# Two layers of a hybrid attention trunk on one core: the dilated blocks taken two together, their scores four blocks ahead, and the output weights' splitting pinned behind the gates

## The chip, the cores and the metric

The kernel runs on one core of one Trainium2 chip. The metric is the device time in microseconds (us) of one execution. The engines are named as in the profile: PE is TensorE (PEld its weight loads), DVE is VectorE, ACT is ScalarE, POOL is GpSimd, and SP is SyncE, which here only issues DMAs. Each engine runs its own instructions in a fixed order and waits by semaphores for the others.

## The reference

What is computed, cut to what matters here (2048 positions, width 1024, two layers, float32):

```python
for layer in range(DEPTH):
    h = _rmsnorm(x, norm_g[layer])
    proj = einsum('bsd,dc->bsc', h, w_in[layer])
    qa, ka, va, ga, qd, kd, vd, gd = split(proj, cuts)
    oa = _stick_breaking(qa, ka, va) * silu(ga)          # 4 heads of 64
    qd, kd = rope(rmsnorm(qd)), rope(rmsnorm(kd))         # 12 heads of 64
    od = _dilated_mixture(qd, kd, vd) * silu(gd)
    x = x + concat([oa, od]) @ w_out[layer]

def _dilated_mixture(q, k, v):       # patterns (window, dilation): (128,1), (512,4), (2048,16)
    for window, dilation in DIL_PATTERNS:
        # blocks of 128 queries; keys: the block itself and the one before it
        s = q_block @ k_two_blocks / 8, masked to 0 <= dist <= window // dilation
        m = max(s); p = exp(s - m); l = sum(p)
        o = (p @ v_two_blocks) / l; log_den = m + log(l)
    alpha = softmax(stack(log_dens)); return sum(alpha * stack(outs))
```

## The kernel before

Each layer goes through four stages: the input projection, the stick-breaking heads, the dilated heads, and the output projection, which also begins the next layer. Matmuls that have to be exact split a float32 operand into a rounded part and the rest (cast, subtract) and add three products.

**The dilated stage** works on 6 pairs of heads. A pair has 48 blocks of 128 queries, 16 for each of the three patterns. In the first pattern, and for the first block of a sequence in the others, the keys are 128 wide, otherwise 256. A block `g` goes through three steps.

- `front(g)`: four score matmuls (L742) into one of the banks 0 to 2, then for each of two heads the mask and maximum on DVE (L744, out of the bank into a page of SBUF) and the exponential with its sum on ACT (L748).
- `mid(g)`: two or four transposes on PE (L763) into bank 3 or 4, then one copy to SBUF (L765), by ACT for `g % 4 == 1`, else by DVE.
- `back(g)`: once in four blocks, the products with the values (L777) into bank 5 and a copy by ACT into the pair's result page `o3` (L782, L784 or L787, by pattern).

The loop over `g` writes `front(g + 3)` ahead of `mid(g)`, and `back(g - 4)` behind it. PE's order is that of the program, since its instructions are pinned; on the other engines a scheduler decides where an instruction stands, by times of its own.

Beside this runs the mixing of the pair before. `stats_a` and `stats_b` (at `t = 1` and `t = 5`, where `t` is the block within the pair) make weights out of the three patterns' maxima and sums: five small POOL operations, one reciprocal on DVE (L832), four more on POOL (L833 to L836), which end in the tile `wr`. `weigh` then multiplies 128 positions by their weights: a matmul that reads `wr` (L847, called W below) and one DVE operation on its bank (L848). It is done for 16 chunks, one in each block from `t = 17`. `gate` adds the patterns and multiplies by the gate for four chunks at a time (three POOL operations of 128x512, L855, L856, L858), and `put` (L866) writes them to `mixa_l` in DRAM. Of the last pair, stats, weigh and gate follow only when all blocks are done, with the stats on DVE.

**The output stage** reads 7 of the 8 rows of `mixa_l` in slices of 128 positions (`load_m`: a DMA, L954, a cast on ACT, L957, and a subtract on DVE, L958) and multiplies them by the split output weights (L963, L966, L967; the three are called a step below). The weights come in 16 pieces of 128x512. `split(i)` casts a piece (L928; POOL for the first six, else ACT) and subtracts (L929, POOL). The first eight are loaded during the last blocks of the dilated stage; the other eight go into the page `G0`, which holds the `o3` of the last pair but one until its last `put` has landed (L945). The first two slices' steps fill PE until the last pair's `wr` is there: the first W of the last pair stands behind 12 steps.

## Time and profile before

| | |
|---|---|
| three runs, median (lowest, highest) | 3153.92 us (3147.05, 4272.47) |
| the profiled execution, its own time | 3151.59 us |
| its span, first to last instruction | 3149.9 us |
| mean granted TensorE clock, share of full | 0.993 |
| PE, DVE, ACT, POOL busy | 97%, 49%, 44%, 37% of the span |
| dilated stage, layer 0 and layer 1 | about 978 to 1376 us and 2545 to 2946 us |

The shares of the table are means over stages that have different limits. A timeline row gives the start, the length, the engine, the line, the tiles written and read, and in brackets how long the engine had been idle before it and what released it. PE's matmuls overlap, so the distance from one start to the next says what one costs, not its own length. The granted clock is 1.00 at 2.4 GHz and 0.50 at 1.2 GHz.

### The profile page before, as it was taken

To read this page: it belongs to the slowest core of one execution; us is meant where nothing else is said; L and a number is where in the kernel's file an instruction comes from. 1 tells how busy PE (TensorE), PEld (TensorE's weight loads), DVE (VectorE), ACT (ScalarE), POOL (GpSimd) and SP (SyncE) were. 2 spreads that over 40 slices of the span, in tenths; PEclk is the share of its full clock that TensorE was granted. 3 is DMA by queue.
4 is the path that set the end of the run, shared out by engine and by line. 5 is a ranking of instruction groups with operands and counts; after the bars stand their busy time and mean duration, and the time that the engine had idled before them with its cause. 6 is when DMAs were issued, how large, how long until landed. Compare 5 with 4: busy or idle time off the path is not lost.

```text
span 3149.9 us, 58168 instructions
## 1 busy us (share of the span) xinstructions
PE 3069.2 (97%) x21328; PEld 2615.0 (83%) x21328; DVE 1551.8 (49%) x4035; ACT 1370.4 (44%) x3917; POOL 1170.3 (37%) x1302
## 2 busy tenths in 40 slices
PE   8999999999999999979999999999999999999799
PEld 8888888887778988868898888888877789888687
DVE  6234430013777878864253243301147778888621
ACT  5222221113667888852042122211136688888410
POOL 1056651102663445451010666511036624445500
PEclk9999999999999999989999999999999999999899
DMA  6234456417123566354343344563172236663443
GB/s 200 89 102 121 112 137 199 136 53 227 58 81 95 154 192 176 104 163 145 124 144 104 97 110 119 148 205 119 59 219 61 72 95 177 190 174 102 137 146 99
DMA packets 316891, 413.10 MB, mean 131 GB/s; under 512 B 23232, under 2 KB 248512, under 8 KB 306368
## 3 DMA queue, kind: packets, MB, share of 16 engines
q1 hardware_dynamic: 314304, 405.20, 44.0%
q10 hardware_dynamic: 2304, 4.20, 0.4%
q8 instruction: 170, 2.79, 0.4%
q14 instruction: 113, 0.93, 0.1%
HBM read 252.01 MB, written 157.29 MB: 130 GB/s over the span
## 4 chain that ended last, share of the span: by engine, by line
PE 82%; issue 6%; ACT 4%; DVE 3%; DMA 2%; POOL 2%; SPq 1%; DVEq 0%; POOLq 0%; ACTq 0%
PE b L742 8%; PE b L317 7%; PE b L316 7%; PE b L315 7%; PE b L777 6%; PE b L763 6%; PE b L321 6%; PE b L323 6%; PE b L322 6%; PE b L599 4%; PE b L967 4%; PE b L966 4%; PE b L963 4%; PE b L585 2%; PE b L558 2%
## 5 line engine op out<-in xcount | busy, mean ns | idle before, releaser
L748 ACT ACTIVATE H<-H,T 128x256 f32<-128x256 f32 (+1 forms) x1152 | 519.4, 455 | 74.3 <-DVE T L744 67.8
L744 DVE CUSTOM_DVE_ANT_0 H<-b,M 128x256 f32<-128x256 f32 (+1 forms) x1152 | 370.9, 360 | 110.7 <-PE b L742 41.5
L742 PE MATMUL b<-F,F 128*128 128x256 f32 (+1 forms) x2304 | 408.4, 301 | 3.1 <-DVE T L744 3.1
L317 PE MATMUL b<-F,F 128*128 128x512 f32 (+1 forms) x1152 | 410.0, 356 | 0.5 <-DVE F L288 0.3
L573 POOL TENSOR_TENSOR G<-G 128x512 f32<-128x512 f32 (+3 forms) x320 | 287.7, 911 | 196.5 <-DVE G L567 143.2
L567 DVE TENSOR_TENSOR_SCAN G<-G,b 128x513 f32<-128x513 f32 (+3 forms) x320 | 323.8, 1079 | 73.2 <-ACT G L566 68.1
L742 PEld LDWEIGHTS b<-F,F 128*128 128x128 f32 x2304 | 312.1, 191 | 32.1 <-issue 26.3
L763 PE MATMUL b<-ident,H 128*128 128x128 f32 x1800 | 298.8, 277 | 7.8 <-ACT H L765 5.4
L315 PE MATMUL b<-F,G 128*128 128x512 f32 (+1 forms) x768 | 275.7, 359 | 0.4 <-ACT G L287 0.4
L316 PE MATMUL b<-F,G 128*128 128x512 f32 (+1 forms) x768 | 273.6, 356 | 1.5 <-POOL F L218 1.5
L315 PE MATMUL b<-F,F 128*128 128x512 f32 (+1 forms) x768 | 274.1, 357 | 0.0
L316 PE MATMUL b<-F,F 128*128 128x512 f32 (+1 forms) x768 | 272.3, 355 | 0.0
L317 PEld LDWEIGHTS b<-F,F 128*128 128x128 f32 x1152 | 217.6, 189 | 32.2 <-DVE F L288 1.1
L765 DVE COPY H<-b 128x512 f32<-128x512 f32 (+1 forms) x432 | 241.2, 558 | 4.3 <-PE b L763 4.1
L777 PE MATMUL b<-H,H 128*64 128x128 f32 x3600 | 235.7, 278 | 0.1
L763 PEld LDWEIGHTS b<-ident,H 128*128 128x128 f32 x1800 | 212.2, 141 | 17.7 <-ACT H L765 7.7
L322 PE MATMUL b<-F,F 128*128 128x512 f32 x576 | 224.6, 390 | 0.0
L566 ACT ACTIVATE G<-b 128x512 f32<-128x512 f32 (+3 forms) x320 | 163.9, 559 | 132.3 <-PE b L559 105.9
L777 PEld LDWEIGHTS b<-H,H 128*64 128x64 f32 x3600 | 192.8, 137 | 32.2 <-issue 21.9
L748 ACT ACTIVATION_READ_ACCUMULATOR H<-H,T 128x1 f32 x1152 | 219.5, 191 | 0.0
L135 POOL TENSOR_SCALAR U<-U 128x16 f32<-128x16 f32 (+1 forms) x80 | 18.9, 236 | 536.8 <-DVE U L367 316.3
L963 PE MATMUL b<-F,H 128*128 128x512 f32 x448 | 179.4, 400 | 29.3 <-ACT H L957 29.3
(159 smaller groups left out, 6297.0 us busy)
## 6 DMA issues: line engine op xcount, KB each, us to landing
qk_l<-H SPq DMA_DIRECT2D x384, 128.0 KB
F<-qk_l SPq DMA_DIRECT2D x48, 1024.0 KB
v_l<-S SPq DMA_DIRECT2D x288, 128.0 KB
H<-v_l SPq DMA_DIRECT2D x72, 512.0 KB
F<-qk_l SPq DMA_DIRECT2D x48, 512.0 KB
sq_l<-H SPq DMA_DIRECT2D x64, 256.0 KB
g_l<-S SPq DMA_DIRECT2D x64, 256.0 KB
F<-sq_l SPq DMA_DIRECT2D x32, 512.0 KB
```

The costliest lines, as they stand in the source:

```text
L315: nc.tensor.matmul(ps, hT(q, 0, k)[:, cs], wh, start=k == 0, stop=False)
L316: nc.tensor.matmul(ps, hT(q, 0, k)[:, cs], wl, start=False, stop=False)
L317: nc.tensor.matmul(ps, hT(q, 1, k)[:, cs], wh, start=False, stop=k == NK - 1)
L322: nc.tensor.matmul(ps, wh[:, w], hT(tq, 1, k), start=False, stop=False)
L567: nc.vector.tensor_tensor_scan(out=r[:, 0:n + 1][:, ::-1], data0=g[:, 512 - n:513][:, ::-1], data1=z[:, 0:1].to_broadcast([128, n + 1]), i ...
L573: nc.gpsimd.tensor_tensor(out=b[:, :n], in0=r[:, 1:n + 1], in1=r[:, 0:n], op=ALU.subtract)
L742: pin(nc.tensor.matmul(sc[:, h, :un], qb, kv, start=s == 0, stop=s == 1))
L744: nc.vector.tensor_tensor_reduce(out=pe[:, h, :un], in0=sc[:, h, :un], in1=mk[:, m0:m0 + un], scale=-0.125, scalar=3.0e38, op0=ALU.add, op ...
L748: nc.scalar.activation(pe[:, h, :un], pe[:, h, :un], AF.Exp, scale=-1.0, bias=st[:, 0, p, h, b:b + 1], accum_out=st[:, 1, p, h, b:b + 1])
L763: pin(nc.tensor.transpose(tp[:, ch, h], pe[:, h, 128 * w:128 * w + 128], ident))
L777: pin(nc.tensor.matmul(ob[64 * h:64 * h + 64, b % 4], vq[(pr * 3 + p) * 2 + (b - ch) // 8][:, (b - ch) % 8, 64 * h:64 * h + 64], ts[:, ch, h],
L963: ins = nc.tensor.matmul(ps, h, wo[k][:, 0, ns], start=k == 0, stop=False)
```

## The change

The loop of the dilated stage takes two blocks at a time: two `front`, four blocks ahead now; then W; then `back`, now ahead of `mid`; then two `mid`. In the first pattern the two blocks' transposes share one bank and one copy. The pages for the exponentials are six instead of five, those for the transposed ones four instead of five. W goes by a new timetable, with three chunks in four blocks (`t = 16` to 36), and for the last pair but one two in every two blocks (`t = 18` to 32). Gates follow their fourth chunk at once, and puts have new times.

In the output stage the six splits on POOL and all subtracts are pinned in the program's order. The first `load_m` is issued ahead of the late weights and its split ahead of theirs. The late weights come in another order, and the first steps take `k` 0 to 3 for both halves before `k` 4 to 6. Of the last pair's gates, those that DVE does are now the first and the third.

```diff
-    pe_s = Slices([pa[:, 0], pa[:, 1], pb[:, 0], pb[:, 1], tb[:, 512:1024].rearrange("p (h k) -> p h k", h=2)])
+    pe_s = Slices([pa[:, 0], pa[:, 1], pb[:, 0], pb[:, 1]]
+                  + [tb[:, i:i + 512].rearrange("p (h k) -> p h k", h=2) for i in (0, 512)])
...
-    ts_s = Slices([td[:, 0], td[:, 1], ta[:, 0], ta[:, 1], tb[:, 0:512].rearrange("p (c h q) -> p c h q", c=2, h=2)])
+    ts_s = Slices([td[:, 0], td[:, 1], ta[:, 0], ta[:, 1]])
...
     def mid(g):
...
+        both = g // 16 % 3 == 0
+        for i in range(2):
+            first = geom(g // 16 % 3, g % 16 + i)[2]
+            pe = pes.pop(g + i)
+            if i == 0 or not both:
+                tp, ts = t_r.get([128, 2, 2, 128]), ts_s.get()
...
+            if both and i == 0:
+                continue
+            on_act = g % 8 == 2 if both else (g + i) % 4 == 1
+            (nc.scalar.copy if on_act else nc.vector.tensor_copy)(ts[:, :lo + nch], tp[:, :lo + nch])
...
-        e1 = nc.vector if final and c4 % 2 else nc.gpsimd
+        e1 = nc.vector if final and c4 % 2 == 0 else nc.gpsimd
...
-    LEAD = 3
+    LEAD = 4
...
-        if g + LEAD < total:
-            front(g + LEAD)
-        if pr and 17 <= t < 33:
-            weigh(pr - 1, t - 17)
-            if t % 4 == 0:
-                gate(pr - 1, (t - 17) // 4)
-        mid(g)
-        if g % 4 == 0 and g:
-            back(g - 4)
+        if g % 2 == 0:
+            for i in (0, 1):
+                if g + LEAD + i < total:
+                    front(g + LEAD + i)
+            if pr:
+                cs = range(t - 18, t - 16) if pr == NPAIR - 1 else range(3 * (t - 16) // 4, 3 * (t - 14) // 4)
+                for c in cs:
+                    if 0 <= c < NT:
+                        weigh(pr - 1, c)
+                        if c % 4 == 3:
+                            gate(pr - 1, c // 4)
+            if g % 4 == 0 and g:
+                back(g - 4)
+            mid(g)
...
-            elif t in (26, 30, 34, 38):
-                put(pr - 1, (t - 26) // 4)
+            elif pr == NPAIR - 1 and t in (27, 31, 35, 38):
+                put(pr - 1, (t - 27) // 4 if t < 38 else 3)
+            elif pr < NPAIR - 1 and t in (25, 31, 35, 41):
+                put(pr - 1, (t - 25) // 5)
...
+    late = (8, 10, 12, 9, 11, 13, 14, 15)
...
+        if k < 3:
+            tc.keep_in_program_order(nc.gpsimd.tensor_copy(w[:, 0, ns], raw))
+        else:
+            nc.scalar.copy(w[:, 0, ns], raw)
+        tc.keep_in_program_order(nc.gpsimd.tensor_tensor(out=w[:, 1, ns], in0=raw, in1=w[:, 0, ns].bitcast(F32),
+                                                         op=ALU.subtract))
...
+    ms = [load_m(0)]
+    for j, i in enumerate(late):
+        raws[i] = ar[:, 2048 + 512 * j:2560 + 512 * j]
+        nc.sync.dma_start(out=raws[i], in_=w_l[:, i // 2, 512 * (i % 2):512 * (i % 2) + 512])
+    ms.append(load_m(1))
     yield
-    for i in range(8, 16):
+    m7 = yield
+    hl = [split_m(ms[0])]
+    for i in late:
         split(i)
-    m7 = yield
-    if proj:
-        proj.begin()
+    hl.append(split_m(ms[1]))
...
+        for ks in ((0, 1, 2, 3), (4, 5, 6)):
+            for n in range(2):
+                if ks[0] == 0:
+                    early[c, n] = acc.get([128, 512])
+                for k in ks:
+                    mms(early[c, n], mh, ml, c, k, slice(512 * n, 512 * n + 512), True)
+                    yield
+    if proj:
+        proj.begin()
```

In the changed file the lines have other numbers: scores L743, mask L745, exponential L749, transposes L767, their copy L772, products with the values L783, the copies into `o3` L790 and L793, reciprocal L838, the POOL operations behind it L839 to L842, W L853 and its DVE operation L854, gate L862 to L864, put L872, weight split L943, L945 (cast on POOL, on ACT) and L946, `load_m` L951, its cast and subtract L957 and L958, late weights L976.

**The first W of a pair.** On PE, in pair 1 of layer 0, the first W of pair 0 (its tile is read as `W`) stood behind one block's scores, before:

```order
L763 MATMUL b_1083_9625<-ident,H_772_7472 128x128 x2
...
L777 MATMUL b_1084_9629<-H_771_7471,H_1041_9350 64x128 x4
L742 MATMUL b_1085_9639<-F_949_8670,F_1003_9054 128x128
...
L847 MATMUL b_1087_9650<-W_7475,F_900_8376 128x384
L763 MATMUL b_1088_9653<-ident,H_769_7469 128x128 x4
L742 MATMUL b_1090_9661<-F_949_8670,F_1003_9054 128x256
```

After, it stands behind the scores of the blocks 20 and 21 (banks `b_1067` and `b_1068`) and ahead of the products with the values and the next transposes:

```order
L767 MATMUL b_1062_9577<-ident,H_770_7470 128x128 x4
L743 MATMUL b_1067_9593<-F_942_8663,F_996_9047 128x128
...
L743 MATMUL b_1068_9602<-F_942_8663,F_996_9047 128x256
...
L853 MATMUL b_1070_9613<-W_7475,F_900_8376 128x384
L783 MATMUL b_1071_9616<-H_771_7471,H_1033_9341 64x128 x8
L767 MATMUL b_1072_9626<-ident,H_772_7472 128x128 x2
L767 MATMUL b_1073_9630<-ident,H_772_7472 128x128 x4
```

On DVE, at the same pair, the reciprocal stood ahead of the masks of the blocks 12 to 20, with the first W's operation (L848 on bank `b_1087`) behind them, before:

```order
L765 COPY H_773_7473<-b_1060_9489 128x256
L832 RECIPROCAL X_7474<-X_7474 32x128
L744 ISA H_769_7469,T_1028_9254<-b_1062_9503,M_7467 128x128
...
L765 COPY H_772_7472<-b_1083_9625 128x256
...
L848 TENSOR_TENSOR G_905_8389<-G_905_8389,b_1087_9650 128x3x128
```

After, it stands behind the mask and maximum of block 21 (bank `b_1068`), and the next row is that W's operation (on bank `b_1070`):

```order
L772 COPY H_771_7471<-b_1062_9577 128x512
L745 ISA H_770_7470,T_1018_9214<-b_1067_9593,M_7467 128x128
...
L745 ISA H_770_7470,T_1018_9214<-b_1068_9602,M_7467 128x256
L745 ISA T_1018_9214 128x1
...
L838 RECIPROCAL X_7474<-X_7474 32x128
L854 TENSOR_TENSOR G_905_8389<-G_905_8389,b_1070_9613 128x3x128
L772 COPY H_773_7473<-b_1072_9626 128x256
```

So the reciprocal has come to the block whose scores stand right ahead of W on PE. It is the same in the pairs 3 and 5 (there one block later) and in both layers; in the pairs 2 and 4 it stands behind block 13, eight blocks ahead.

**The end of the dilated stage, POOL and SP.** On POOL, in layer 0, the gates of pair 4 (`G_1474`, the `o3` of that pair) stood among the splits of the weights, before:

```order
L855 TENSOR_TENSOR G_1474_12277<-G_1474_12277 128x512
L929 TENSOR_TENSOR F_1761_14229<-F_1741_14069,F_1761_14229 128x512
L929 TENSOR_TENSOR F_1750_14140<-F_1740_14064,F_1750_14140 128x512 x2
...
L858 TENSOR_TENSOR G_1474_12277<-G_1474_12277,S_1707_13854 128x512
L929 TENSOR_TENSOR F_1755_14176<-F_1741_14069,F_1755_14176 128x512
L856 TENSOR_TENSOR G_1474_12277<-G_1474_12277 128x512
L858 TENSOR_TENSOR G_1474_12277<-G_1474_12277,S_1722_13948 128x512
L496 MEMSET T_2378_20806 128x128
```

After, the four gates (now `G_1440`) stand ahead of all splits:

```order
L864 TENSOR_TENSOR G_1440_12189<-G_1440_12189,S_1664_13793 128x512
L862 TENSOR_TENSOR G_1440_12189<-G_1440_12189 128x512
L863 TENSOR_TENSOR G_1440_12189<-G_1440_12189 128x512
L864 TENSOR_TENSOR G_1440_12189<-G_1440_12189,S_1678_13885 128x512
L943 CAST F_1697_14002<-F_1695_13991 128x512
L946 TENSOR_TENSOR F_1697_14002<-F_1695_13991,F_1697_14002 128x512
...
L946 TENSOR_TENSOR F_1714_14142<-F_1696_13996,F_1714_14142 128x512 x2
L946 TENSOR_TENSOR F_1733_14290<-G_1719_14177,F_1733_14290 128x512
```

On SP, the two `load_m` stood behind the late weights, before:

```order
L866 DMA mixa_l_205<-G_1474_12277 128x512
L844 DMA S_1792_14455<-g_l_204 128x512
...
L635 DMA M_22679<-in_masks 128x732
L945 DMA G_1766_14264<-in_w_out 128x512 x8
L954 DMA G_1766_14264<-mixa_l_205 128x7x128 x2
L257 DMA X_14400<-in_norm_g 128x1024
```

After, the first stands ahead of them and the next behind, with the next layer's weights (L214) last:

```order
L872 DMA mixa_l_205<-G_1440_12189 128x512 x3
L850 DMA S_1741_14352<-g_l_204 128x512
L951 DMA G_1719_14177<-mixa_l_205 128x7x128
L976 DMA G_1719_14177<-in_w_out 128x512 x8
L951 DMA G_1719_14177<-mixa_l_205 128x7x128 x2
L214 DMA H_1767_14486<-in_w_in 128x4x256
...
L850 DMA S_1747_14384<-g_l_204 128x512
```

**The end of the dilated stage, ACT.** The end of ACT's row in layer 0, before, with the last exponentials ahead of all that waits for the late weights or for `mixa_l`:

```order
L748 ACTIVATE H_770_7470,T_1624_13286<-H_770_7470,T_1624_13286 128x256 x2
L787 COPY G_1623_13285<-b_1769_14288 128x4x16x8
L765 COPY H_773_7473<-b_1770_14306 128x512
L787 COPY G_1623_13285<-b_1773_14324 128x4x16x8
L820 COPY X_7474<-b_1777_14350 32x384
L217 CAST F_1784_14402<-H_1787_14408 128x1024
L820 COPY X_7474<-b_1778_14359 32x384
L217 CAST F_1784_14402<-H_1786_14404 128x1024
L828 ACTIVATE X_7474<-X_7474 32x384
L928 CAST F_1779_14380<-G_1766_14264 128x512 x2
```

After, the cast of the first slice and casts of late weights (`G_1719` is the page that the DMAs fill) stand among the exponentials of the last four blocks:

```order
L957 CAST H_1731_14286<-G_1719_14177 128x896
L945 CAST F_1733_14290<-G_1719_14177 128x512
L749 ACTIVATE H_770_7470,T_1582_13182<-H_770_7470,T_1582_13182 128x256 x4
L793 COPY G_1581_13181<-b_1711_14110 128x4x16x8
L945 CAST F_1733_14290<-G_1719_14177 128x512
L772 COPY H_773_7473<-b_1713_14134 128x512
L749 ACTIVATE H_772_7472,T_1582_13182<-H_772_7472,T_1582_13182 128x256 x3
L945 CAST F_1736_14305<-G_1719_14177 128x512
...
L945 CAST F_1734_14293<-G_1719_14177 128x512 x2
L772 COPY H_773_7473<-b_1722_14212 128x512
L793 COPY G_1581_13181<-b_1725_14230 128x4x16x8
L957 CAST H_1737_14310<-G_1719_14177 128x896
```

So on ACT the work that waits for DMAs has moved from behind the last copies to ahead of them.

## Rows read from the trace of the kernel before

**Rows 1.** The page: busy time of each engine, share of the span.

```profile
PE 3069.2 (97%) x21328; PEld 2615.0 (83%) x21328; DVE 1551.8 (49%) x4035; ACT 1370.4 (44%) x3917; POOL 1170.3 (37%) x1302
```

**Rows 2.** Stages: length, busy us of PE, PEld, DVE, ACT, POOL, then PEclk.

```profile
1126.70:1142.60 15.90, 15.90 (x155) 14.58 (x154) 15.13 (x60) 13.55 (x51) 6.65 (x6) 1.00 0.47 152
1376.00:1402.00 26.00, 8.48 (x32) 6.18 (x32) 10.22 (x14) 10.11 (x15) 11.30 (x10) 0.61 0.95 306
2946.00:2965.00 19.00, 6.47 (x18) 4.52 (x17) 8.37 (x13) 7.71 (x12) 11.68 (x8) 0.64 0.94 295
```

**Rows 3.** Timeline, PE, layer 1, last pair: start, length, line, idle before.

```profile
2919.87 0.79 PE L742 MATMUL b<-F,F 128*128 128x256 f32 x4
2920.49 0.60 PE L763 MATMUL b<-ident,H 128*128 128x128 f32 x4
2920.85 0.78 PE L742 MATMUL b<-F,F 128*128 128x256 f32 x4
2924.08 1.12 PE L763 MATMUL b<-ident,H 128*128 128x128 f32 x4 [2.45 <-ACT H L765]
2924.85 1.20 PE L742 MATMUL b<-F,F 128*128 128x256 f32 x4
2925.85 1.05 PE L763 MATMUL b<-ident,H 128*128 128x128 f32 x4
```

**Rows 4.** Timeline, ACT, the same stretch.

```profile
2920.94 0.62 ACT L928 CAST F<-F 128x512 fp32r<-128x512 f32 x1 [2.71 <-DMA F<-in_w_out]
```

**Rows 5.** Timeline, PE, end of the dilated stage of layer 0.

```profile
1393.85 0.77 PE L963 MATMUL b<-F,H 128*128 128x512 f32 x1 [16.96 <-ACT H L957]
...
1405.91 0.39 PE L967 MATMUL b<-F,H 128*128 128x512 f32 x1
1406.14 0.34 PE L847 MATMUL b<-W,F 128*128 128x384 f32 x1
```

**Rows 6.** Timeline, SP, the same end.

```profile
1375.76 0.46 SPq L866 DMA_DIRECT2D mixa_l<-G  x1
...
1381.24 3.79 SPq L945 DMA_DIRECT2D G<-in_w_out  x8
1385.17 1.52 SPq L954 DMA_DIRECT2D G<-mixa_l  x2
```

**Rows 7.** Timeline, POOL, the same end.

```profile
1366.34 1.29 POOL L858 TENSOR_TENSOR G<-G,S 128x512 f32<-128x512 f32 x1
...
1385.88 8.72 POOL L929 TENSOR_TENSOR F<-G,F 128x512 fp32r<-128x512 f32 x7 [9.16 <-ACT F L928]
```

**Rows 8.** Timeline, PE, end of the dilated stage of layer 1.

```profile
2958.76 0.77 PE L963 MATMUL b<-F,H 128*128 128x512 f32 x1 [12.33 <-ACT H L957]
...
2970.15 0.34 PE L847 MATMUL b<-W,F 128*128 128x384 f32 x1
```

**Rows 9.** Timeline, SP, the same end.

```profile
2936.44 10.34 SPq L844 DMA_DIRECT2D S<-g_l  x2
```

**Rows 10.** Timeline, DVE, layer 0, statistics of pair 0, in pair 1.

```profile
1118.96 0.94 DVE L832 RECIPROCAL X<-X 32x128 f32<-32x128 f32 x1 [1.42 <-POOL X L831]
```

**Rows 11.** Timeline, POOL, after that row.

```profile
1119.98 0.99 POOL L833 TENSOR_TENSOR X<-X 32x384 f32<-32x384 f32 x1 [1.05 <-DVE X L832]
...
1124.79 0.50 POOL L836 CAST W<-X 32x384 fp32r<-32x384 f32 x1
```

**Rows 12.** Timeline, PE, after that row.

```profile
1121.51 1.10 PE L777 MATMUL b<-H,H 128*64 128x128 f32 x16
1122.53 0.66 PE L742 MATMUL b<-F,F 128*128 128x128 f32 x4
...
1127.18 0.39 PE L847 MATMUL b<-W,F 128*128 128x384 f32 x1
```

**Rows 13.** Timeline, DVE, end of the dilated stage of layer 0.

```profile
1385.07 0.35 DVE L834 CAST W<-X 32x384 fp32r<-32x384 f32 x1
...
1386.03 1.32 DVE L836 CAST W<-X 32x384 fp32r<-32x384 f32 x1
```

More of the change, by code (lines that the diff above doesn't have):

```diff
@@ L919, in _output, with load_m, split_m @@
     acc = mem.bank_ring(0, 1, 2, 5)
-    wo, raws = [], []
+    wo, raws = {}, {}
     pages = ("F0", "F1", "F2", "F3", "F9", "F10", "F11", "F8")
+    late = (8, 10, 12, 9, 11, 13, 14, 15)
     def split(i):
         k, ns = i // 2, slice(512 * (i % 2), 512 * (i % 2) + 512)
-        if i % 2 == 0:
-            wo.append(mem.get(pages[k], [128, 2, DM], F32R))
+        if k not in wo:
+            wo[k] = mem.get(pages[k], [128, 2, DM], F32R)
         w, raw = wo[k], raws[i]
-        (nc.gpsimd.tensor_copy if k < 3 else nc.scalar.copy)(w[:, 0, ns], raw)
-        nc.gpsimd.tensor_tensor(out=w[:, 1, ns], in0=raw, in1=w[:, 0, ns].bitcast(F32), op=ALU.subtract)
+        if k < 3:
[4 more added lines that the diff above has]
+                                                         op=ALU.subtract))
+    def load_m(c):
+        m = m_s.get()
+        nc.sync.dma_start(out=m[:, 0:7], in_=mix[0][:, :, 128 * c:128 * c + 128].rearrange("k p t -> p k t"))
+        return m
+    def split_m(m):
+        mh = mh_r.get([128, 8, 128], F32R)
+        ml = ml_r.get([128, 8, 128], F32R)
+        nc.scalar.copy(mh[:, 0:7], m[:, 0:7])
+        nc.vector.tensor_tensor(out=ml[:, 0:7], in0=m[:, 0:7], in1=mh[:, 0:7].bitcast(F32), op=ALU.subtract)
+        return mh, ml
     for j in range(8):
@@ L967, in mms @@
         nc.tensor.matmul(ps, l, wo[k][:, 0, ns], start=False, stop=k == 7)
[L969 removed]
+    early = {}
     for c in range(2):
[L971 to L976 removed]
+        mh, ml = hl[c]
+        for ks in ((0, 1, 2, 3), (4, 5, 6)):
[7 more added lines that the diff above has]
+        proj.begin()
     for c in range(NT):
[L978 to L979 removed]
+        mh, ml = hl[c] if c < 2 else split_m(load_m(c))
         xt = x_s.get()
```

51 lines of the change are left out of this document (13 added, 38 removed).

## The prediction

> **What bounds the kernel now.** I read the page first: PE is busy 97% of the span, every other engine under half of it, PEld apart [rows 1]. So nothing that another engine saves counts unless PE waits for it. Next I read the stages, to find where PE does not work: 26 us after the dilated stage of layer 0 hold 8.48 us of PE at a granted clock of 0.61, and 19 us in layer 1 hold 6.47 at 0.64 [rows 2]. Then the timeline of PE inside the dilated stage: score matmuls and transposes alternate with 0.62 us from scores to transposes and 0.36 back [rows 3]. There PE is bound by its own issue, and what can be gained is the small waits and the alternation. The rest (the projection, the stick-breaking heads, most of the output) the change does not touch.
>
> **The end of the dilated stage (gain).** PE's last work before the gap ends at 1393.85 - 16.96 = 1376.89 us in layer 0; call it Z. The first W of the last pair starts at 1406.14, Z + 29.25 [rows 5]. In layer 1, Z is 2958.76 - 12.33 = 2946.43 and that W starts at Z + 23.72 [rows 8]. Ahead of that W stand 12 steps of three matmuls, 0.23 us apart at full clock [rows 5], 0.70 a step, 8.4 us in all. The rest is waiting and half clock. The chain in layer 0: the last gate ends at 1367.6, since splits lie between the gates [rows 7]; its put is issued at 1375.76, the late weights at 1381.24, the first slice only at 1385.17 [rows 6], and PE starts on its cast. In layer 1 SP stands in one issue from 2936.44 for 10.3 us ahead of all that [rows 9].
>
> After, the last gate has no split ahead of it. It takes three operations of 1.29 us [rows 7] behind a W that PE issues 12 blocks ahead of the end, and by my estimate (1.0 to 1.5 us a block, as the starts in rows 3 have it) it is done 14 us ahead of Z. A put then took 5.5 us until what waits for its landing was issued [rows 6]; with that and some 4 us for the slice, which now stands ahead of the late weights on SP, the slice has landed 4.5 to 7 us ahead of Z. So PE goes from the stats to the steps without a gap, and W of the last pair would start at Z + 8.4 in layer 1. In layer 0 ACT has two casts of the next layer's weights, whose DMAs are now issued last, ahead of the last pair's exponential; by my estimate W starts at Z + 11.1. Gains: 29.25 - 11.1 = 18.2 and 23.72 - 8.4 = 15.3, together 33.5 us. The half clock goes with the gap.
>
> **The same end (cost).** ACT works in order, and six casts of late weights and the cast of the first slice now stand ahead of the last exponentials and copies. Each waits for a DMA. The trace has such a wait: a cast waited 2.71 us for its weights, and PE sat idle 2.45 us for it [rows 3, 4]. With the slice landing 4.5 to 7 us ahead of Z and the weights behind it, the exponentials of the last four blocks come 2 to 4 us late. I take 3.0 us for each layer (between 0 and 6): 6.0 us. Net of the end: -27.5 us.
>
> **The first W in the pairs 1, 3 and 5 (cost).** This is the new wait. The reciprocal stands on DVE behind the mask of block 21 (22 in pair 5), and PE has W directly behind the scores of that block. Between them lie the last masks' end on DVE, the reciprocal, 0.94 us [rows 10], and four POOL operations, two of 1.0 and two of 0.5 us (one of each is shown) [rows 11]: 0.94 + 3.0 = 3.94, and with some 1.3 us for the two masks and the hand-overs 5.2 us; in pair 5, where PE has other work meanwhile, I take 4.7. What is queued behind W on PE is everything: products, transposes, the next scores. DVE stands behind it too, with W's own operation. Before, nothing waited there: `wr` was ready at 1124.79 + 0.50 and the first W came at 1127.18 [rows 11, 12]. Per layer 5.2 + 5.2 + 4.7 = 15.1 us, 30.2 in both.
>
> The clock follows. After 2.45 us of idle PE the same work took 0.77 instead of 0.36 us and 1.00 instead of 0.62 [rows 3]: two fifths of the stretch were lost. How long a spell lasts behind a longer gap no row here says to the microsecond; I take between 3.4 and 7 us behind each of the six waits, 1.3 to 2.9 us lost, 1.8 taken: 10.8 us.
>
> **The flow of the blocks (gain).** Taking two blocks together halves the changes between scores and transposes, from eight to four in four blocks. A round of scores and transposes takes 0.98 us, though four scores alone last 0.78 and four transposes 0.60 [rows 3], so they overlap and a change can cost little: I take 0.025 us (between 0 and 0.07), 0.10 for four blocks, 1.0 for the most of a pair. In the second pattern DVE is at 15.13 of 15.90 us [rows 2], and with three W in four blocks instead of four it has a quarter of its W operations less there; I take 1.0 us of PE's time for a pair (between 0 and 1.5). The reciprocal's wait before, for which DVE sat idle 1.42 us [rows 10], is gone in pairs 1, 3 and 5; of it and the reciprocal's 0.94 us I take 0.5 us as seen by PE. So -2.5 us for each of these; in pairs 2 and 4 the reciprocal stays and blocks DVE for as long as before, with the copies of two blocks behind it: -1.1; in pair 0, with no W and no reciprocal, -1.0. Per layer 3 x 2.5 + 2 x 1.1 + 1.0 = 10.7, in both 21.4 us.
>
> Edits with no price: the pages (one more for exponentials, one less for transposed blocks) only serve the order; the new puts stand on SP behind no DMA that PE waits for before the end; the shared copy of the first pattern saves DVE work in a stretch where PE waits for ACT and itself. ACT would then be nearly as full as PE there; if it does not keep up, the first pattern gives back some 0.3 us a pair.
>
> **A term the trace does not show.** Products now follow scores directly. No row has that sequence. The nearest is the reverse: 16 products and then scores take 1.02 us from start to start [rows 12], and at 0.055 us a product, from their length in the row, the last of them costs 0.20 us until the scores start. I take that for the new sequence, with bounds 0.09 below and above it. There are 144 of these in the run, so -13 to +13 us, 0 taken.
>
> **Sum.** -27.5 + 30.2 + 10.8 - 21.4 = -7.9 us against the profiled run's own 3151.6: 3143.7, say 3144. That run lies 2.3 us below the median of the three; I make no correction for it.
>
> **Rivals.** (1) *No wait at the first W.* If the weights are ready when PE comes to W, the two W terms vanish: 3151.6 - 27.5 - 21.4 = 3103. For it: the W of before had 1.9 us to spare, and a stall lets ACT catch up, which may return some of it. Against it: the order on PE, DVE and POOL is fixed, and the reciprocal stands behind the mask that itself waits for PE's last scores ahead of W. Chance 0.18.
>
> (2) *Slower: products behind scores are dear.* The place is each `back`, 144 times. At 0.29 us instead of 0.20 the flow's gain shrinks by 13 us and the time is 3157. It decides from 0.20 + 7.9 / 144 = 0.26 us on: beyond that the kernel is slower than before. For it: products and transposes read other pages and another format than the scores, and each change in PE's order seen so far costs something. Against it: the reverse costs 0.20 [rows 12]. Chance 0.13.
>
> (3) *POOL holds DVE at the end.* A cast of the stats on DVE that took 0.35 us took 1.32 when a row of POOL's subtracts began just ahead of it [rows 7, 13]. After, the late subtracts run on POOL from just ahead of Z to some 10 us behind it, and the last pair's stats, some eight DVE operations, fall in that time; if each second one loses 1 us, W of the last pair comes 4 us late in each layer, and the time is 3152, no change at all. For it: the row. Against it: in layer 0 most subtracts should be over by then. Chance 0.14. The Trainium skill, "SBUF — State Buffer", section "SBUF: two separate sides", has the rule for this: DVE and POOL share a port pair as an exclusive lock, and whichever starts first keeps it for the whole instruction. The row agrees with it (0.97 us lost, less than POOL's 1.29). It speaks against a change that gathers POOL's splits; by it the sum would be some 8 us higher, without it nothing.
>
> **How the numbers follow.** The forecast has 0.55 with a range of its own of 3130 to 3157. The range of 8 in 10 has to reach down into rival 1, at 3103 give or take 10, and up over rival 2: 3094 to 3166. A change of 2% is 63 us, about what a measurement of this kernel tells from none; 3091 and 3217 are the limits. Faster by more needs rival 1 with the end at its best (-33.5): 0.05. Slower by more needs all costs at their upper bounds and more: 0.02. Within: 0.93.
>
> **What would show it.** In the trace after: the first W (L853) of pairs 1, 3 and 5 with 4 to 6 us idle ahead of it, released by POOL L842, and a granted clock under 1 behind it; in pairs 2 and 4 none. PE idle under 2 us at Z, no stretch at 0.5 there, W of the last pair at Z + 8 to 11. Casts L945 and L957 on ACT waiting for DMAs ahead of the last exponentials, with PE idle 2 to 4 us ahead of Z. Pairs 2 and 4 shorter by some 1 us each. Wrong it would be above all if the first slice lands later than I reckon, for then the last exponentials, and all behind them, wait for it.

## The result, and the profile after

The changed kernel takes 3174.78 us (median of four runs, 3169.09 to 3180.91) against 3149.19 for the one before (median of three); the ratio is 1.0079, with an interval of 1.0052 to 1.0106. It is slower by 0.8%, where 3144 was forecast with a range that ended at 3166. A fourth run of before, at 4272.47 us, was a slow one and stands outside this comparison, though the median of 3153.92 in the table ahead still counts it. The profiled execution of after took 3175.19 us with a span of 3173.5, 23.6 more than the span before.

The page of after, busy time of each engine [rows 1 were before]:

```profile
PE 3071.5 (97%) x21328; PEld 2628.6 (83%) x21328; DVE 1545.8 (49%) x3963; ACT 1360.1 (43%) x3893; POOL 1172.8 (37%) x1302
```

PE is busy for 2.3 us more, the span is 23.6 longer: the rest, 21.3 us, is idle PE. So the list of PE's waits of after comes next (total, times, longest in us):

```profile
PE b L853 <- POOL W L842: 31.7, 6, 5.6
PE b L767 <- ACT H L772: 11.3, 10, 3.4
...
PE b L853 <- DVE W L842: 7.9, 2, 5.0
PE b L783 <- DMA H<-v_l: 5.4, 1, 5.4
```

Before, the head of this list was L963 on L957, 29.3 us in two waits, the gaps of [rows 5, 8]; that line is gone. The first line is the forecast wait at the first W of the pairs 1, 3 and 5 (30.2 us forecast). The second stood at 5.4 us before, so it has grown by 5.9. The third and the fourth were not in the forecast's sum.

**The first W**, pair 1 of layer 0, timeline of PE, DVE and POOL. (The captions of [rows 10 to 12] say pair 1; those rows lie in pair 2, which begins at 1102.6 us. The argument is the same in each pair.)

```profile
1057.85 1.17 PE L743 MATMUL b<-F,F 128*128 128x128 f32 x8
1064.65 0.69 PE L853 MATMUL b<-W,F 128*128 128x384 f32 x1 [5.62 <-POOL W L842]
1065.26 1.98 PE L783 MATMUL b<-H,H 128*64 128x128 f32 x16
1067.17 1.54 PE L767 MATMUL b<-ident,H 128*128 128x128 f32 x6
```

```profile
1060.42 0.94 DVE L838 RECIPROCAL X<-X 32x128 f32<-32x128 f32 x1
```

```profile
1053.53 2.29 POOL L687 CAST F<-F 128x512 fp32r<-128x512 f32 x4
1055.78 0.44 POOL L837 TENSOR_TENSOR X<-X 32x128 f32<-32x128 f32 x1
1061.43 0.98 POOL L839 TENSOR_TENSOR X<-X 32x384 f32<-32x384 f32 x1 [5.21 <-DVE X L838]
...
1064.10 0.49 POOL L842 CAST W<-X 32x384 fp32r<-32x384 f32 x1
```

The reader is to see two things. The reciprocal had its input at 1056.2 and stood ready for 4.2 us behind masks; then the chain over POOL takes 3.2 us, with PE behind it. And ahead of L837 POOL ran four casts of the third pattern's queries, 2.29 us together, which the forecast did not look at.

The stretch behind this wait, a window of after (length, busy us of PE, PEld, DVE, ACT, POOL, then PEclk):

```profile
1064.60:1068.60 4.00, 3.95 (x24) 3.30 (x25) 0.98 (x2) 0.59 (x1) 0.00 (x0) 0.50 0.03 7
```

The granted clock fell to 0.50, its lower level, behind the 5.62 us of idle PE. The 16 products behind W take 1.91 us there from their start to the next, where 16 took 1.02 in [rows 12].

**Pair 3 of layer 0.** PE's timeline, the chain of waits ahead of it (start, length, what), and SP's timeline; below them the row of SP for the same load before:

```profile
1198.66 1.73 PE L783 MATMUL b<-H,H 128*64 128x128 f32 x13 [5.43 <-DMA H<-v_l]
```

```profile
1175.93 22.59 DMA H<-v_l
```

```profile
1171.26 0.32 SPq L663 DMA_DIRECT2D F<-qk_l  x1
1171.67 0.45 SPq L664 DMA_DIRECT2D F<-qk_l  x1
1172.17 2.54 SPq L665 DMA_DIRECT2D F<-qk_l  x1
1174.81 0.54 SPq L663 DMA_DIRECT2D F<-qk_l  x1
1175.40 0.45 SPq L664 DMA_DIRECT2D F<-qk_l  x1
1175.93 0.54 SPq L697 DMA_DIRECT2D H<-v_l  x1
1176.52 9.64 SPq L665 DMA_DIRECT2D F<-qk_l  x1
```

```profile
1168.20 1.51 SPq L696 DMA_DIRECT2D H<-v_l  x1
```

The load of the values for pair 3 stands on SP behind five of the six loads of queries and keys; before it stood behind three. It is issued 69.5 us behind the start of pair 2, where it was 65.6. It took 22.59 us to land, and PE waited for it.

**The end**, both layers, timeline of PE. The steps now follow the statistics without a gap (Z is 1405.15 and 2984.39), but W waits behind them:

```profile
1405.15 0.50 PE L987 MATMUL b<-F,H 128*128 128x512 f32 x1
...
1418.82 0.66 PE L853 MATMUL b<-W,F 128*128 128x384 f32 x1 [5.01 <-DVE W L842]
...
2984.39 0.50 PE L987 MATMUL b<-F,H 128*128 128x512 f32 x1
...
2995.99 0.42 PE L853 MATMUL b<-W,F 128*128 128x384 f32 x1 [2.93 <-DVE W L842]
```

So W comes at Z + 13.7 and Z + 11.6, instead of Z + 29.25 and Z + 23.72 [rows 5, 8]. POOL and DVE at the same place in layer 0, to be read against [rows 7, 13]:

```profile
1380.54 1.27 POOL L864 TENSOR_TENSOR G<-G,S 128x512 f32<-128x512 f32 x1
...
1409.58 8.30 POOL L946 TENSOR_TENSOR F<-G,F 128x512 fp32r<-128x512 f32 x6 [4.90 <-ACT F L945]
```

```profile
1411.32 1.26 DVE L836 TENSOR_TENSOR X<-X 32x128 f32<-32x128 f32 x1
1412.61 1.26 DVE L837 TENSOR_TENSOR X<-X 32x128 f32<-32x128 f32 x1
1413.91 0.94 DVE L838 RECIPROCAL X<-X 32x128 f32<-32x128 f32 x1
...
1415.46 1.30 DVE L840 CAST W<-X 32x384 fp32r<-32x384 f32 x1
1416.80 1.50 DVE L841 TENSOR_TENSOR X<-X,W 32x384 f32<-32x384 f32 x1
```

POOL's row of six subtracts lies over the last pair's statistics, and four of DVE's operations take 1.26 to 1.50 us. The loads, SP, against [rows 6]:

```profile
1385.62 0.37 SPq L951 DMA_DIRECT2D G<-mixa_l  x1
1386.04 4.60 SPq L976 DMA_DIRECT2D G<-in_w_out  x8
```

The last gate now ends 23 us ahead of Z, at 1381.8 (forecast: 14; before: 9), and the first slice is issued at 1385.62, ahead of the late weights.

Ahead of Z, PE waits for ACT, whose copy stands behind exponentials and casts, in layer 1 (PE, then ACT):

```profile
2973.48 0.91 PE L767 MATMUL b<-ident,H 128*128 128x128 f32 x4 [3.41 <-ACT H L772]
```

```profile
2967.51 0.94 ACT L957 CAST H<-G 128x896 fp32r<-128x896 f32 x1 [1.66 <-DMA G<-mixa_l]
2969.36 0.62 ACT L945 CAST F<-G 128x512 fp32r<-128x512 f32 x1 [0.90 <-DMA G<-in_w_out]
...
2972.32 0.62 ACT L945 CAST F<-G 128x512 fp32r<-128x512 f32 x1
2972.84 0.58 ACT L772 COPY H<-b 128x512 f32<-128x512 f32 x1
```

So this row of ACT begins with two waits for DMAs, 1.66 us for the slice and 0.90 for a late piece. In layer 0 PE waits 2.40 us at 1381.55 for a copy in the same way, and there ACT had waited for one of the first eight pieces:

```profile
1375.46 0.62 ACT L945 CAST F<-F 128x512 fp32r<-128x512 f32 x1 [2.48 <-DMA F<-in_w_out]
```

The length of a pair in us, from the start of its first score to that of the next pair's first (pair 5: to that of its last row of scores), from the timelines of PE. The last column belongs to a run told below (e13), in which no W of these pairs is waited for:

| pair | before, layer 0, 1 | after, layer 0, 1 | e13, layer 0, 1 |
|---|---|---|---|
| 0 | 58.15, 58.19 | 56.30, 56.30 | 56.25, 56.28 |
| 1 | 66.37, 66.69 | 72.33, 72.65 | 64.73, 64.78 |
| 2 | 66.67, 66.40 | 65.83, 66.59 | 64.71, 64.71 |
| 3 | 66.38, 66.69 | 80.07, 72.95 | 64.71, 65.00 |
| 4 | 66.68, 66.43 | 65.83, 66.52 | 64.73, 64.91 |
| 5 | 65.58, 67.67 | 75.65, 73.16 | 70.14, 66.30 |

### The profile page after: what moved, and what is told of

It reads as the page before. It is cut to its first block, busy times and chain, and to the rows that moved or that the text cites. A ratio compares the mean times of both kernels' runs of the same rounds, so it can differ in the third digit from the quotient of the medians.

```text
span 3173.5 us, 57966 instructions
## 1 busy us (share of the span) xinstructions
PE 3071.5 (97%) x21328; PEld 2628.6 (83%) x21328; DVE 1545.8 (49%) x3963; ACT 1360.1 (43%) x3893; POOL 1172.8 (37%) x1302
## 4 chain that ended last, share of the span: by engine, by line
PE 86%; ACT 5%; DVE 4%; issue 2%; POOL 2%; DMA 2%; SPq 0%; DVEq 0%; ACTq 0%; POOLq 0%
PE b L317 9%; PE b L316 9%; PE b L315 9%; PE b L743 7%; PE b L783 6%; PE b L767 6%; PE b L321 6%; PE b L323 6%; PE b L322 6%; PE b L599 4%; PE b L991 4%; PE b L990 4%; PE b L987 4%; PE b L585 2%; ACT H L749 2%
## 5 line engine op out<-in xcount | busy, mean ns | idle before, releaser
L749 ACT ACTIVATE H<-H,T 128x256 f32<-128x256 f32 (+1 forms) x1152 | 518.0, 452 | 111.0 <-DVE T L745 110.8
L745 DVE CUSTOM_DVE_ANT_0 H<-b,M 128x256 f32<-128x256 f32 (+1 forms) x1152 | 353.0, 361 | 47.7 <-PE b L743 31.7
L743 PE MATMUL b<-F,F 128*128 128x256 f32 (+1 forms) x2304 | 349.2, 296 | 2.8 <-DVE T L745 2.7
L743 PEld LDWEIGHTS b<-F,F 128*128 128x128 f32 x2304 | 299.3, 195 | 6.1 <-DVE T L745 3.8
L772 DVE COPY H<-b 128x256 f32<-128x256 f32 (+1 forms) x360 | 223.7, 641 | 107.2 <-PE b L767 106.9
L767 PE MATMUL b<-ident,H 128*128 128x128 f32 x1800 | 262.8, 283 | 12.3 <-ACT H L772 11.3
L783 PE MATMUL b<-H,H 128*64 128x128 f32 x3600 | 237.3, 283 | 10.2 <-DMA H<-v_l 5.4
L317 PEld LDWEIGHTS b<-F,F 128*128 128x128 f32 x1152 | 217.5, 189 | 31.5 <-DVE F L288 0.3
L767 PEld LDWEIGHTS b<-ident,H 128*128 128x128 f32 x1800 | 201.7, 143 | 45.6 <-issue 25.3
L783 PEld LDWEIGHTS b<-H,H 128*64 128x64 f32 x3600 | 199.8, 140 | 33.9 <-issue 20.5
L749 ACT ACTIVATION_READ_ACCUMULATOR H<-H,T 128x1 f32 x1152 | 217.1, 188 | 0.0
L488 DVE TENSOR_TENSOR S<-b,S 128x512 f32<-128x512 f32 x64 | 44.3, 692 | 319.3 <-ACT S L487 304.3
```

Source lines behind the costliest of these rows:

```text
L317: nc.tensor.matmul(ps, hT(q, 1, k)[:, cs], wh, start=False, stop=k == NK - 1)
L743: pin(nc.tensor.matmul(sc[:, h, :un], qb, kv, start=s == 0, stop=s == 1))
L745: nc.vector.tensor_tensor_reduce(out=pe[:, h, :un], in0=sc[:, h, :un], in1=mk[:, m0:m0 + un], scale=-0.125, scalar=3.0e38, op0=ALU.add, op ...
L749: nc.scalar.activation(pe[:, h, :un], pe[:, h, :un], AF.Exp, scale=-1.0, bias=st[:, 0, p, h, b:b + 1], accum_out=st[:, 1, p, h, b:b + 1])
L767: pin(nc.tensor.transpose(tp[:, lo + ch, h], pe[:, h, 128 * w:128 * w + 128], ident))
L772: (nc.scalar.copy if on_act else nc.vector.tensor_copy)(ts[:, :lo + nch], tp[:, :lo + nch])
```

## The experiments

Theory at the start: the two W terms and rival 3 are real, and both can be taken away by where things stand in order. Rival: the loop by two blocks costs by itself. Each time below is a median with the ratio to before and its interval; differences against after are worked out from the medians.

**The loop and the output apart.** The old loop with the changed output stage (e4):

> The dilated stage of the kernel before with the changed output stage: it leaves the two-together loop out. Theory: the changed end is worth 10 to 18 us by itself, and the loop is what makes the changed kernel slower: 3134 to 3142 us. Rival (the end's change loses by itself what POOL holds back, and the loop is neutral): 3150 us or more.

Measured 3130.66 us, 0.9936 [0.9921, 0.9951], 3 us under the theory's range. And the changed loop with the old output stage (e8):

> The changed loop with the output stage of the kernel before. If the two parts add (output -19 us by the fourth run, both together +24): loop +43, 3192 us, 3184 to 3199. If they interact, so that the changed output is what lengthens the changed loop's last pair: 3175 to 3184.

Measured 3191.36, 1.0130 [1.0115, 1.0145], as expected if the parts add. Against the runs of before beside them the output part gains 19 us and the loop loses 42; their sum, 24 us, is about what was measured together (25.6 by the medians, 23.6 by the spans). The loss is the loop's.

**W later.** W, gates and puts of the pairs 1 to 4 come four blocks later (e1):

```diff
-    ... else range(3 * (t - 16) // 4, 3 * (t - 14) // 4)
+    ... else range(3 * (t - 20) // 4, 3 * (t - 18) // 4)
-            elif pr < NPAIR - 1 and t in (25, 31, 35, 41):
+            elif pr < NPAIR - 1 and t in (29, 35, 39, 45):
```

> The changed kernel with W, gates and puts of the pairs 1 to 4 four blocks later (the last pair's timetable as it was); the reciprocal then stands two to ten masks ahead of the first W's own operation in every pair. Theory (the first W waits for the reciprocal's place in DVE's order): all six waits of 4.6 to 5.6 us go, 31.7 us, and the half-clock spells behind them, some 4 us: 3139 us, 3133 to 3147. Rival (DVE is so full in the second pattern that the work it caught up with during the waits has to be done anyway): at most half comes back, 3155 to 3160.

Measured 3194.4, 1.0141 [1.0122, 1.0160], a miss by 55 us and the slowest of all, though W's wait fell to 4.0 us, nearly as expected. The timeline of PE, then of ACT, pair 2:

```profile
1127.39 1.98 PE L783 MATMUL b<-H,H 128*64 128x128 f32 x16 [6.31 <-ACT G L788]
```

```profile
1126.75 0.58 ACT L788 COPY G<-b 128x512 f32<-128x512 f32 x1 [7.51 <-DMA mixa_l<-G]
```

The next pair's first result copy needs the page `o3`, of which there are two, and that page is free only when the last put has landed. The wait moved there: 47.6 us in eight.

**The late weights in another order.** The order of `late` decides which cast comes last on ACT, and so what POOL's pinned row waits for (e2):

```diff
-    late = (8, 10, 12, 9, 11, 13, 14, 15)
+    late = (8, 9, 14, 15, 10, 11, 12, 13)
```

> The changed kernel with the late weights in the order 8, 9, 14, 15, 10, 11, 12, 13 of pieces, in which ACT can cast them, so that POOL's pinned subtracts do not wait for a cast that ACT does last. Theory (a row of six POOL subtracts falls on the last pair's stats and holds DVE's operations, which come out at 1.3 us instead of 0.3 to 0.55): two instead of six are left there, the first W of the last pair waits 0 to 1.5 us instead of 5.0 and 2.9, no half clock behind it: 3164 to 3168 us. Rival (the stats start late because ACT's exponential stands behind casts that wait for the next layer's weights): layer 0 keeps its wait, 3172 to 3175.

Measured 3165.63, 1.0045 [1.0030, 1.0060]. POOL, DVE and PE of this run, layer 0:

```profile
1404.61 2.85 POOL L946 TENSOR_TENSOR F<-G,F 128x512 fp32r<-128x512 f32 x2 [4.04 <-ACT F L945]
```

```profile
1406.35 1.26 DVE L836 TENSOR_TENSOR X<-X 32x128 f32<-32x128 f32 x1
1407.65 0.28 DVE L837 TENSOR_TENSOR X<-X 32x128 f32<-32x128 f32 x1
```

```profile
1410.98 0.41 PE L853 MATMUL b<-W,F 128*128 128x384 f32 x1 [1.27 <-DVE W L842]
```

An addition of the same size on DVE takes 1.26 us beside POOL's row and 0.28 behind it (L837 itself: 1.26 in the changed kernel, 0.28 here); with two subtracts there instead of six, W's wait goes from 7.9 us in both layers to 1.3. Rival 3 is shown. The 9 us between this run and the changed kernel are not all of this kind, though: of the 11.1 us between the two profiled runs 6.4 lie in the pairs 0 to 4 of layer 0, nearly all in pair 3, where the wait for the load of values is absent in this run. With W later as well (e3):

> Both edits together. If the two causes are separate, the gains add: 3129 us, 3122 to 3138, faster than the kernel before by 0.5 to 1%. If they share a cause (both waits only make room for work that is due anyway): 3145 to 3155.

Measured 3186.46, 1.0105 [1.0089, 1.0122], the same miss: 52.3 us in waits for `o3`, as in e1. With the old loop (e6):

> The loop of the kernel before, the changed output stage, and the late weights in the order of the second run. Theory (POOL's row of subtracts holds DVE's stats of the last pair there too): the two waits of 2.4 us at the last pair's first W and the half clock behind them go, 5 to 8 us: 3123 to 3127 us, the fastest so far. If POOL is not what holds them: 3130, as without.

Measured 3120.91, 0.9909 [0.9894, 0.9923], 2 us under the expected range; no W waits at the end. Here the order of `late` is worth 9.8 us against e4, with the pairs 0 to 4 as long as there.

**What in the output gains.** Of the change, only the pinning of the splits in the old kernel (`keep_in_program_order` on them, as in the diff of the change, and nothing else; e10):

> The kernel before with the splits' pins alone (POOL's six casts and all subtracts); loads, order of pieces and steps as before. Theory (the last gate and put stood behind the splits, so that everything behind the put came late): the put lands some 15 us sooner and most of the output's gain is here: 3131 to 3140 us. Rival (the slice behind the late weights is what PE waits for): 3142 to 3149.

Measured 3128.91, 0.9933 [0.9918, 0.9947], 2 us under the expected range and no less a gain than the whole output part. Only the first slice's load moved ahead of the late weights (e11):

```diff
+    m0 = m_s.get()
+    nc.sync.dma_start(out=m0[:, 0:7], in_=mix[0][:, :, 0:128].rearrange("k p t -> p k t"))
     for i in range(8):
...
-        m = m_s.get()
-        nc.sync.dma_start(out=m[:, 0:7], in_=mix[0][:, :, 128 * c:128 * c + 128].rearrange("k p t -> p k t"))
+        m = m0 if c == 0 else m_s.get()
+        if c:
+            nc.sync.dma_start(out=m[:, 0:7], in_=mix[0][:, :, 128 * c:128 * c + 128].rearrange("k p t -> p k t"))
```

> The kernel before with the first slice's DMA alone issued ahead of the late weights. By the rows of before, the slice would land some 5 us sooner, but the steps from k = 4 on then wait for the late weights' subtracts: 2 to 5 us a layer: 3139 to 3146 us. By the rival of the run with the pins alone: 3130 to 3138.

Measured 3137.44, 0.9960 [0.9946, 0.9974], a little under the expected 3139 to 3146 and within its rival's range, so the slice's place gains something by itself. Its list of PE's waits still has the cast of the slice, 18.0 us instead of 29.3:

```profile
PE b L966 <- ACT H L960: 18.0, 2, 11.2
```

The slice cannot come sooner than the last gates, and these stand among the splits as long as nothing pins them.

**The reciprocal's place.** Masks and reciprocal are pinned on DVE, the reciprocal behind the mask 17 (`pin` keeps the program's order; `rest` is the reciprocal and the four operations behind it; e5):

```diff
-            nc.vector.tensor_tensor_reduce(
+            pin(nc.vector.tensor_tensor_reduce(
...
-        nc.vector.reciprocal(mn, mn)
+        def rest():
+            pin(nc.vector.reciprocal(mn, mn))
...
+            elif t == 12:
+                rest()
```

> The changed kernel in which only the reciprocal's place on DVE is fixed: the masks and the reciprocal are pinned, and the reciprocal with the four POOL operations behind it is written at block 12, so that it stands behind the mask of block 17 in every pair. W keeps its timetable. Theory (the place in DVE's order is the whole cause of the six waits): they shrink from 4.6 to 5.6 us to 0 to 1.5, no half clock behind them: 3143 us, 3137 to 3150. Rival (the loop taken two together is slow by itself, and the waits only took up that time): above 3160.

Measured 3166.09, 1.0047 [1.0030, 1.0065], a miss by 23 us. The lists of PE's waits say why:

```profile
PE b L855 <- POOL W L843: 14.3, 8, 1.9
...
PE b L743 <- DVE T L745: 9.5, 10, 2.3
```

The wait is shared between W and the masks, since the reciprocal's input is not there sooner: L837 ends 22 us behind the pair's first scores. With the late weights' order as well (e7):

> The changed kernel with the reciprocal's place fixed and the late weights reordered. Theory (the two-together loop gains nothing by itself, since a change between scores and transposes costs nothing): 3134 us, 3128 to 3141, which is the old loop's time with the same output stage plus 3 to 12 us. Rival (the flow gains the 10 us a layer that were forecast, once the waits are gone): 3115 or less.

Measured 3156.59, 1.0023 [1.0013, 1.0033], above theory (by 22 us) and rival: the same two waits (14.6 and 10.4 us). With the reciprocal two blocks later, W from `t = 20`, two chunks in two blocks, and the puts moved to suit (e9):

> The changed kernel with three mends: the reciprocal pinned behind the mask of block 19 or 20, W of the pairs 1 to 4 from t = 20 on with two in every two blocks and puts at 27, 31, 35 and 39, and the late weights reordered. Theory (the waits at the first W are all that the two-together loop loses; it needs 0.6 us a pair less than the old loop, 1.9 in pair 0): no wait of PE at W, pairs 1 to 5 near 65.9 us: 3112 us, 3104 to 3121, as fast as or faster than the old loop with the same output stage (3121). Rival (loads or pages come late in the new loop whatever W does, as the waits for v_l in some runs): 3128 to 3145.

Measured 3141.90, 0.9971 [0.9960, 0.9982], a miss by 30 us and in its rival's range, though by another cause: W's wait 5.2 us, the masks' 17.9. A reciprocal that waits among masks is a wait of PE, as the banks of the scores are emptied by DVE alone.

**The chain's place on POOL.** First the wrong way round, the query casts (L687) pinned ahead of the whole chain, the reciprocal pinned at `t = 8`, and the late weights' other order (e12):

> The changed kernel with its first-W chain brought forward: the split casts of the following queries (L687, GpSimd) stand behind the statistics no more but ahead of them, the reciprocal is written eight blocks into the pair and kept in place behind the first 14 mask operations on DVE, and the last layer-end casts go 9th, then 14th and 15th as in the run with the later casts. W and gates keep the changed kernel's timetable. Theory (what the changed kernel loses is the wait of PE for the first W of a pair, and the reciprocal is to blame only through where it stands; four blocks of lead let DVE wait there without emptying the score banks): no row 'PE b L853 <- POOL W' above 5 us in all and no wait of PE on the masks above 5 us, pairs 1 to 5 at 65 to 67 us, pair 0 at 56.3, time 3108 to 3122. Rival (a reciprocal that waits among the masks empties the score banks wherever it stands): 'PE b L743 <- DVE T L745' at 9 to 18 us in 10 waits, time 3135 to 3150. Second rival (the chain is late whatever is done, its casts being held by other work): W wait 12 us and more, time 3145 to 3160.

Measured 3190.16, 1.0129 [1.0112, 1.0146]; all three expectations missed. DVE, then PE:

```profile
1057.42 0.94 DVE L839 RECIPROCAL X<-X 32x128 f32<-32x128 f32 x1 [5.93 <-POOL X L837]
```

```profile
1058.78 1.22 PE L743 MATMUL b<-F,F 128*128 128x256 f32 x4 [6.30 <-DVE T L745]
```

The casts of the second head's queries start only 19.5 us into the pair, so a chain behind them is later, not sooner, and a reciprocal placed early stops all masks for 5.93 us: the masks' wait is 63.5 us. It showed the lever, though: the chain had to go ahead of these casts. So, with the chain L833 to L843 pinned ahead of them, the casts written at `t = 14`, the reciprocal behind the 16th mask, and the late weights' other order (e13; against e12, without the pins):

```diff
-        if t == 2:
+        if t == 14:
             make_q(pr, 2)
...
-            elif t == 8:
+            elif t == 11:
                 rest()
```

> The changed kernel with the last layer-end casts late and, on GpSimd, the whole chain to the first W (L833 to L843) kept in place ahead of the eight casts of the third pattern's queries (L687), which are written 12 blocks later; the reciprocal is kept in place on DVE behind the first 16 masks. W, gates and puts keep the changed kernel's timetable. In the changed kernel L837 ended 22.1 us behind a pair's first scores, with four L687 casts of 2.29 us in all ahead of it; without them it should end at 19.8, the reciprocal run right then behind the sixteenth mask, and the weights be there at 24.4, while PE comes to W at 24.9. Theory (the chain's place on POOL and DVE is all that the changed loop loses, and taking two blocks together gains next to nothing by itself): W waits under 2 us and mask waits under 5 us in all, pairs 1 to 5 at 65.5 to 66.8 us, pair 0 at 56.3, time 3113 to 3125, the same as the old loop with the changed output (3121). Rival (the loop gains what the prediction had, and the waits hid it): pairs 63 to 65, time 3095 to 3110. Second rival (a chain is late in this loop wherever it stands): W or mask waits above 12 us, time above 3135.

Measured 3107.34 us, 0.9868 [0.9852, 0.9885], faster than both kernels and than any other run. POOL, DVE and PE in pair 1, whose first scores start at 1029.7:

```profile
1049.21 0.45 POOL L837 TENSOR_TENSOR X<-X 32x128 f32<-32x128 f32 x1
...
1053.68 0.50 POOL L843 CAST W<-X 32x384 fp32r<-32x384 f32 x1
1054.24 4.64 POOL L687 CAST F<-F 128x512 fp32r<-128x512 f32 x8
```

```profile
1049.96 0.94 DVE L839 RECIPROCAL X<-X 32x128 f32<-32x128 f32 x1
```

```profile
1054.49 0.33 PE L855 MATMUL b<-W,F 128*128 128x384 f32 x1
```

L837 ends at 19.9 us, the weights are there at 24.4, W starts at 24.8, all as expected, and no wait stands at these W, nor at the masks beyond 0.2 us. The pairs 1 to 4 take 64.7 to 65.0 us and the time is the rival's too: with its chain in place the loop does gain, 1.5 to 2.0 us a pair against before, and the waits hid it. The theory's "next to nothing" fell. Against the old loop with the same output (3121) it is 14 us faster; the changed loop as it was, with the same output (3166), is 45 slower. The old loop was not run with the chain pinned and the casts moved, so a part of the 14 us could be these edits' own. It can be only a small one: in the pairs 1 to 4 of e6 PE is idle for 0.2 to 0.7 us a pair, and more than that no shorter wait can give back.

## Why the prediction was wrong

The sum went by these terms (us, both layers; measured in the profiled runs, the flow by the pairs of e13 where a wait hides it; an asterisk marks a length corrected by an estimate for work that only changed its place):

| term of the sum | predicted | measured |
|---|---|---|
| W of the last pair sooner behind Z | -33.5 | -27.7 |
| casts ahead of the last exponentials | +6.0 | +9.5* |
| wait for the first W | +30.2 | +31.7 |
| what else is lost around that wait | +10.8 | +12.9 |
| flow, pairs 1, 3, 5 | -15.0 | -10.4* |
| flow, pairs 2, 4 | -4.4 | -1.4 |
| flow, pair 0 | -2.0 | +1.1* |
| load of values in pair 3 | none | +7.7 |
| the rest | 0 | +0.2 |
| sum | -7.9 | +23.6 |

How they are measured: W behind Z from the rows above, (29.25 - 13.7) + (23.72 - 11.6). The casts: pair 5's third pattern is 4.5 and 0.1 us longer than before, and from the last score to Z it is 11.3 and 15.5 us instead of 9.0 and 9.0, 13.4 in all. The W wait from the list; what else is lost is the difference of pairs 1, 3, 5 between after and e13 (44.6 us without pair 5's third pattern and the load) less 31.7. The load: pair 3 against pair 1, 80.07 - 72.33. The line of the rest is what closes the sum.

The asterisks: with scores four blocks ahead instead of three, the transposes of one block and one more group of products are still to be done when the next pair's scores begin. So pair 0 holds 236 products and 134 transposes in each layer, where it held 268 and 138, and pair 5 with the end holds them more: 28 products and two transposes from the third pattern on, the others ahead of it. At 1.02 us for 16 products [rows 12] and 0.36 for four transposes [rows 3] this is an estimated 2.4 us a layer. By their lengths pair 0 gave 3.7 us in both layers, the casts cost 13.4 and the pairs 1, 3 and 5 gave 9.5; with the 4.8, 3.9 and 0.9 us of moved work taken off they are as in the table. The pairs 1 to 4 hold as much as before.

**The failed steps.** Three, of some 8 to 11 us each, all in the same direction.

*The flow.* Forecast at -21.4 us, it gave -10.7. "-2.5 for each of these" was too much for pairs 1, 3 and 5; in pairs 2 and 4 the -1.1 came out as 0.8 less in layer 0 and 0.1 to 0.2 more in layer 1, since the reciprocal still holds the masks there (e13 has 64.7); and pair 0, with "no W and no reciprocal", gained nothing by itself: it is 1.9 us shorter a layer with some 2.4 us less to do, and PE is idle in it for 2.0 us instead of 0.6. The lengths of the patterns (third 23.9 us in e13 and before, first 19.8 and 19.7 to 20.0, second 21.0 and 22.7) must be read with what they hold: the first pattern of a pair now has 16 products and two transposes more than before, some 1.2 us of work, in the same time; the second has 12 products and three W less; the third four products and two transposes less and three W more. So most of the gain seems to lie in the first pattern, where the changes between scores and transposes are halved and two blocks share a copy. Which of the two it is, was not taken apart.

*The end.* "If each second one loses 1 us": rival 3 came true in both layers, 3.9 us lost in four operations in layer 0 (1.26 - 0.28 twice and 0.95 twice, by the run with two subtracts), against the argument that "in layer 0 most subtracts should be over by then". They were not, since POOL's pinned order waited for one cast that ACT does last. W came 2.6 and 3.2 us later behind Z than forecast. The Trainium skill, "SBUF — State Buffer", section "SBUF: two separate sides", says that DVE and POOL share a port pair as a lock, which whichever starts first holds for its whole instruction, where the DVE operation has two SBUF inputs or runs in a two-port mode. The trace agrees: DVE's additions L836 and L837 began while a subtract of POOL ran and took 1.26 us each (a subtract takes 8.30 / 6 = 1.38), the multiply L839 began at 1414.88, ahead of a subtract at 1414.96, and kept its 0.55 us while that subtract took 1.59, and the reciprocal, with one input, took its 0.94 us in the midst of the row.

The casts ahead of the last exponentials cost some 9.5 us, not 6.0. The mechanism was the forecast one: PE waited 2.40 and 3.41 us for ACT's copies, whose row began with casts that waited for DMAs, and the same in e13 (3.46 and 3.11). These waits of PE grew by 5.9 us over before; what the rest is, half clock behind them or the two W more, was not taken apart. In layer 0 it was not the slice, which was there when ACT came to it, but one of the first eight pieces.

*The loads.* "The new puts stand on SP behind no DMA that PE waits for before the end" spoke of the puts alone. The order on SP moved the load of values as well, and that was not looked up: the wait for it cost 7.7 us, once, in layer 0. It comes and goes with the build (waits on `v_l` of 8.0, 5.9, 1.8 and 0 us in e8, e5, e2 and e13); why a load takes 22.59 us to land, no run here settles, and that its later issue is the whole cause is not shown.

**What held.** The wait at the first W: place, releaser, number and size (31.7 for 30.2), on which rival 1 fell. Of the products behind the scores rival 2 fell: the time of the pairs in e13 leaves no room for it. The half clock behind each wait is there. It costs about 2 us: pair 1 less pair 1 of e13 is 7.60 us, less the wait of 5.62 makes 2.0, and W, 16 products, six transposes and eight scores behind the wait take 5.1 us (1064.65 to 1069.73), where the same groups take 0.27, 1.02, 0.63 and 1.05 us, 3.0 in all, at the full clock further on in the same pair and ahead of the wait; 1.8 was taken. Pair 2 hides it in a direct comparison, since its own reciprocal holds the masks (65.83 against 64.71). The gap at Z closed as forecast.

## What to carry to other kernels

When work is moved to an earlier place, follow the whole chain that feeds it over every engine, back to the first instruction, and ask what unrelated work stands in that chain: here four casts on GpSimd, 2.29 us together, ahead of a 0.44 us addition decided, with the reciprocal's place, whether taking two blocks together gained 14 us or lost 45. Six runs moved the wait to the next resource (a page, the masks, the casts) before the chain itself was moved; a wait is only gone when its input is sooner or its reader really later. Pin an order only after looking up which of its inputs comes last: the order of eight numbers in `late` was worth 9.8 us in the old loop. And when a loop runs further ahead, count what a stretch holds before its length is read as a gain.

## What the runs showed of the hardware

In the third pattern halving the changes between scores and transposes has next to no price: that of pair 0, which has no W beside it, became 0.6 us shorter (22.6 for 23.2), and it holds four products and two transposes less, an estimated 0.4 us by [rows 3, 12]. The granted clock of 0.50, half of full, behind 5.62 us of idle PE cost about 2 us: 16 products took 1.91 us there instead of 1.02. A row of POOL's subtracts and short DVE operations held each other up both ways: DVE's additions of 0.28 us took 1.26 when a subtract had begun, and a subtract took 1.59 instead of 1.29 us when DVE's multiply had begun 0.08 us ahead of it.
